# Splitting the last stage's weights during the mLSTM stage of a two-layer decoder trunk

## The chip, the core and the metric

The kernel runs on one core of a Trainium2 chip. The metric is the device time of one execution in microseconds (us). Three runs of the kernel before the change took 2989.78 to 2992.91 us, with a median of 2991.87.

A core has five engines that each work through a queue of their own: TensorE (PE in the profile; its weight loads are PEld), VectorE (DVE), ScalarE (ACT), GpSimd (POOL) and SyncE (SP), which here issues DMA transfers only. POOL issues DMA transfers too. An instruction that must wait holds up all that stands behind it on its engine.

## What is computed

One sequence of 2048 tokens with 1024 channels goes through two layers, `x = x + mixer(rmsnorm(x))`. The first mixer is an mLSTM (4 heads with a matrix memory), the second an RG-LRU (a gated linear recurrence of width 1536). The change concerns two weights of the second: the gates' block-diagonal matrices `w_a`, `w_x` (8 blocks of 192x192 each) and the output matrix `w_out`.

```python
def rglru_mixer(u, w_in, conv_w, conv_b, w_a, b_a, w_x, b_x, lam, w_out):
    xr, g = jnp.split(u @ w_in, [R_WIDTH], axis=-1)
    xc = causal_dwconv(xr, conv_w, conv_b)
    xb = xc.reshape(bsz, s, R_BLOCKS, R_BS)
    r = jax.nn.sigmoid(jnp.einsum('bsnc,ncd->bsnd', xb, w_a).reshape(bsz, s, R_WIDTH) + b_a)
    ig = jax.nn.sigmoid(jnp.einsum('bsnc,ncd->bsnd', xb, w_x).reshape(bsz, s, R_WIDTH) + b_x)
    log_a = -LRU_C * r.astype(jnp.float32) * jax.nn.softplus(-lam.astype(jnp.float32))
    bt = jnp.sqrt(-jnp.expm1(2.0 * log_a)) * (ig * xc).astype(jnp.float32)
    hs = linear_scan(jnp.exp(log_a), bt).astype(u.dtype)
    return (hs * jax.nn.silu(g)) @ w_out
```

## The kernel before

**Split operands.** Every large product is made of three passes on TensorE. An operand is split into a high part, a rounded copy, and a low part, the rest: `split_into` (lines 754 to 763) makes the high part by a cast on ScalarE (L759) and the low part by a subtract on VectorE (L762). The three passes are high by high (L359), low by high (L360) and high by low (L361).

**Stages.** The profile's span runs through four stages. Up to about 1000 us the mLSTM's input projections are made. From about 1000 to 1700 us `phase_a2` (line 773) computes the mLSTM: 4 heads after one another, each in 8 blocks of 256 tokens, some 21 us a block. From about 1670 to 2505 us `phase_b1` computes the output product of the first layer and the input product of the second. From 2505 us to the end `phase_b2` (line 1333) computes the RG-LRU's gates, its scan and its output product, in 4 blocks of 512 tokens.

**The mLSTM stage.** One pass of the main loop (lines 1036 to 1065) handles a block: the norm and finish of the block before it (`norm`, line 1012; `finish`, line 1018), the loads for the block after it, the recurrence over its own two chunks, and the projections to q, k and v of the block after it. The norm takes the factors `frs` from POOL (L1010), scales with them on ScalarE (`hh`, L1014), and TensorE transposes the result (`pt`, L1024). `head_weights` (lines 800 to 823) loads a head's weights for q, k and v as raw tiles (tag `wraw`, two slots, L807) and splits them. q's and k's for the next head are asked for at the end of blocks 3 and 5, v's with the next head's first block. Where a split stands in an engine's queue is decided by the scheduler, which merges these calls. In the order that comes out, the splits of q and k of the next head stand at the turn to it, where the splits of v stand too.

**The last stage.** A block has 8 gate steps of 18 matmuls (`gates`, line 1420) and, 5 steps behind, 24 output steps of 12 matmuls, 3 to each gate step (lines 1341 to 1346). Two gate steps serve a quarter of the block's 1536 channels. For a quarter ScalarE makes the sigmoids (L1435, L1438), the decay and its square (L1442, L1443) and, after the load of another function table, the root (L1463). VectorE makes the scan's input (L1466 to L1470), the scan (L1473) and the product with the branch `g` (L1476). Then the quarter of y is split (L759, L762) for the output steps. The x of a quarter is loaded by `load` (L1409) on SP and split in turn.

The weights come through `fetch` (lines 1353 to 1376). In the first block it loads raw tiles through POOL (L1363), splits them, and stores high and low part side by side to DRAM, `d_gw` for the gates and `d_ow` for the output (L1382, 32 stores). In the other three blocks it loads those stored parts through SP (L1360). Explicit orders put the split of the first gate weight ahead of the last work of the stage before, and the first x ahead of the first output weight. The gate pool has two slots for split tiles and two for raw ones, the output pool four and two.

Of the kernel before, what the change touches and what calls it, by code (L numbers as in the profile page):

```python
# [7 lines left out]
F32 = mybir.dt.float32  # L8
F32R = mybir.dt.float32r
# [5 lines left out]
P = 128  # L15
# [9 lines left out]
KV = DV // P  # L25
# [281 lines left out]
class Trunk:  # L307
# [462 lines left out]
                    self.tc.add_manual_dep(t.ins, f.ins.name, mybir.DependencyInfo(  # L770
                        mybir.DependencyClass.NoSync, mybir.DependencyReason.DATA), reason="order")

    def phase_a2(self, wq, wk, wv, D):
        tc, nc = self.tc, self.nc
        BL = 256
        NB = T // BL
        with ExitStack() as ctx:
            wp = ctx.enter_context(tc.tile_pool(name="w2", bufs=1, reuse_waits="tile"))
# [23 lines left out]
            def head_weights(h, names):  # L802
                w = W.setdefault(h, {})
                for nm in names:
                    src = {"q": wq[h], "k": wk[h], "v0": wv[h, :, :, 0:256], "v1": wv[h, :, :, 256:512]}[nm]
                    raw = wp.tile([P, KV, 256], F32, tag="wraw", name="wraw", bufs=2)
                    nc.sync.dma_start(raw, src)  # L807
                    if nm[0] == "v":
                        j = int(nm[1])
                        if j == 0:  # L810
                            w["v"] = (wp.tile([P, KV, 512], F32R, tag="vwh", name="vwh"),
                                      wp.tile([P, KV, 512], F32R, tag="vwl", name="vwl"))
                        hi, lo = (t[:, :, j * 256:(j + 1) * 256] for t in w["v"])
                    else:
                        pool = ob if h % 2 else wp
                        w[nm] = (pool.tile([P, KV, 256], F32R, tag=nm + "wh", name=nm + "wh"),
                                 pool.tile([P, KV, 256], F32R, tag=nm + "wl", name=nm + "wl"))
                        hi, lo = w[nm]
                    a = self.split_into(hi, lo, raw, "a", "v")
                    if h == 0 and nm[0] == "v":  # L820
                        self.order((self.kT,), a)
                    if h == 0 and nm in "qk":
                        self.order(a, self.tail[-4:])

            def project(h, b):

# [38 lines left out]
                def qk():  # L865
# [32 lines left out]
                    if b == 0:  # L898
                        head_weights(h, ("v0", "v1"))
# [112 lines left out]
            def norm(h, b, S):  # L1012
                rs = S["rs"]
                return [nc.scalar.activation(hn, hn, AF.Identity, bias=rs[:, 1, c:c + 1], scale=rs[:, 0, c:c + 1])  # L1014
                        for c, hn in enumerate(S["hh"])]

            def finish(h, b, S):
                y = lp.tile([P, KV, BL], F32, tag="y", name="y")
                for j in range(2):
                    pt = pr.tile([P, 2, 2, P], F32, tag="r", name="pt")  # L1020
                    for k in range(2):
                        for c in range(2):
                            ks = slice((j * 2 + k) * P, (j * 2 + k + 1) * P)
                            nc.tensor.transpose(pt[:, k, c], S["hh"][c][:, ks], self.ident)  # L1024
                    for k in range(2):
                        kk = j * 2 + k
                        a = nc.scalar.activation(y[:, kk], pt[:, k].rearrange("p c t -> p (c t)"), AF.Copy,
                                                 scale=self.v("nw", h * KV + kk))
                        if (h, b) == blocks[-1]:
                            self.tail.append(a)  # L1030
                nc.vector.tensor_tensor(y, y, S["skx"], op=ALU.add)
                end = (h, b) == blocks[-1]
                nc.vector.tensor_tensor(y, y, S["sz"], op=ALU.mult)
                (nc.sync if end else nc.gpsimd).dma_start(D["y"][h * KV:(h + 1) * KV, :, b * BL:(b + 1) * BL].rearrange("k p t -> p k t"), y)

            blocks = [(h, b) for h in range(H) for b in range(NB)]
            S, steps = project(*blocks[0])
            with tc.high_priority():
                steps[0]()
# [3 lines left out]
            for i, (h, b) in enumerate(blocks):  # L1043
                if i + 1 < len(blocks):
                    Sn, (loads, qk, score, v0, v1) = project(*blocks[i + 1])
                else:
                    Sn, loads = None, lambda: None
                    qk = score = v0 = v1 = loads
                if late:
                    norm(*late)  # L1050
                loads()
                recur(h, b, 0, S)
                if late:
                    finish(*late)
                qk()
                recur(h, b, 1, S)
                score()
                v0()
                v1()
                if b in (3, 5) and h < H - 1:  # L1060
                    head_weights(h + 1, "q" if b == 3 else "k")
                late = (h, b, S)
                S = Sn
            norm(*late)
# [20 lines left out]
                             start=True, stop=True)  # L1085
        return pb

    def phase_b(self, xT, wout, rwin, rgate, rwout, D, outT):
        self.phase_b1(xT, wout, rwin, D)
        self.phase_b2(rgate, rwout, D, outT)  # L1090

    def phase_b1(self, xT, wout, rwin, D):

# [236 lines left out]
                    S.group(W, U, out_of(i, s), {"t2": after_t2, "u21": after_u21})  # L1330
                    U, x1 = V, x3

    def phase_b2(self, rgate, rwout, D, outT):


        tc, nc = self.tc, self.nc
        NT = 12
        with ExitStack() as ctx:
            gp = ctx.enter_context(tc.tile_pool(name="g4", bufs=2, reuse_waits="tile"))
            tp = ctx.enter_context(tc.tile_pool(name="t4", bufs=2, reuse_waits="tile"))  # L1340
            wp = ctx.enter_context(tc.tile_pool(name="w4", bufs=4, reuse_waits="tile"))
            pm = ctx.enter_context(tc.tile_pool(name="psB", bufs=8, space=PSUM, reuse_waits="tile"))
# [10 lines left out]
            def fetch(kind, b, i):  # L1353

                m = 768 if kind == "g" else 512
                pool = gp if kind == "g" else wp
                keep = D["gw" if kind == "g" else "ow"][i]
                if b > 0:
                    both = pool.tile([P, 2 * m], F32R, tag="w" + kind, name="w" + kind)
                    nc.sync.dma_start(both.bitcast(F32), keep)  # L1360
                    return both[:, 0:m], both[:, m:2 * m]
                raw = pool.tile([P, m], F32, tag="wr" + kind, name="wr", bufs=2)
                nc.gpsimd.dma_start(raw, rgate[i // 2, :, i % 2 * 768:(i % 2 + 1) * 768] if kind == "g" else  # L1363
                                    rwout[i % NT, :, i // NT * 512:(i // NT + 1) * 512])
                kept(1)
                both = pool.tile([P, 2 * m], F32R, tag="w" + kind, name="w" + kind)
                a = self.split_into(both[:, 0:m], both[:, m:2 * m], raw, "a", "v")
                if kind == "g" and i == 0:
                    self.order(a, self.tail[-4:])
                if kind == "r" and i == 0:  # L1370
                    self.order(self.first, a)
                stores.append((keep, both))
                if i == (7 if kind == "g" else 23):
                    kept(0)
                return both[:, 0:m], both[:, m:2 * m]
            stores = []

            def kept(n):

                while len(stores) > n:  # L1380
                    keep, both = stores.pop(0)
                    nc.gpsimd.dma_start(keep, both.bitcast(F32))  # L1382

            def weights():

# [237 lines left out]
def trunk_kernel(tc, xT, woq, wxz, wq, wk, wv, wout, rwin, rgate, rwout, vecs, gbias, outT):  # L1623
    with ExitStack() as ctx:
        K = Trunk(ctx, tc, vecs, gbias)
        D = {}
        for n, shape in (("o", [NTC, P, MI]), ("xm", [16, P, T]), ("xc", [16, P, T]), ("sz", [16, P, T]),
                         ("y", [16, P, T]), ("x1", [KD, P, T]), ("xr", [12, P, T]), ("g", [12, P, T]), ("q", [64, P]), ("dec", [64, P]), ("wx", [16, 4, P, 1024]),
                         ("wq", [H, 4, 2, P, 1032]), ("wr", [12, 4, P, 1024]), ("ws", [4, 8, P, 1024]),
                         ("gw", [8, P, 1536]), ("ow", [24, P, 1024])):  # L1630
            D[n] = tc.dram_tile(shape, F32, name="d_" + n)
        K.phase_a1(xT, woq, wxz, wout, D)
        K.phase_a2(wq, wk, wv, D)
        K.phase_b(xT, wout, rwin, rgate, rwout, D, outT)


_INS = ["xT", "woq", "wxz", "wq", "wk", "wv", "wout", "rwin", "rgate", "rwout", "vecs", "gbias"]
# [22 lines left out]
```

## Time and profile before

| | us |
|---|---|
| median of three runs | 2991.87 |
| the profiled execution | 2996.22 |
| its span in the trace | 2994.5 |
| mLSTM stage, window shown below | 1020 to 1700 |
| first gate matmul of the last stage | 2509.48 |
| fourth cast of y in the last stage | 2617.98 |

The profile is of one execution, taken by the hardware's profiler. A grouped row gives the source line, the engine, the operation, the tiles out<-in with their shapes, the count, then the busy time, the mean duration in ns, and the idle time of the engine just before, with what ended it. A row of windows gives, for a stretch, the busy time of each engine with its number of instructions in brackets, the granted TensorE clock as a share of full speed, the share of the DMA engines' time in use, and GB/s. A busy time counts overlapping matmuls once. A row of waits gives who waited for whom, the time in all, how often, and the longest one. A row of transfers gives the tiles, the queue, the count, the KB of one and its median us from issue to landing.

### The profile page before, as it was taken

To read this page: it belongs to the slowest core of one execution; us is meant where nothing else is said; L and a number is where in the kernel's file an instruction comes from. 1 tells how busy PE (TensorE), PEld (TensorE's weight loads), DVE (VectorE), ACT (ScalarE), POOL (GpSimd) and SP (SyncE) were. 2 spreads that over 40 slices of the span, in tenths; PEclk is the share of its full clock that TensorE was granted. 3 is DMA by queue.
4 is the path that set the end of the run, shared out by engine and by line. 5 is a ranking of instruction groups with operands and counts; after the bars stand their busy time and mean duration, and the time that the engine had idled before them with its cause. 6 is when DMAs were issued, how large, how long until landed. Compare 5 with 4: busy or idle time off the path is not lost. (4 is left out here: it accounts for less than half of the span.)

```text
span 2994.5 us, 43193 instructions
## 1 busy us (share of the span) xinstructions
PE 2861.5 (96%) x15442; PEld 2448.8 (82%) x15442; DVE 2127.1 (71%) x3596; ACT 1517.2 (51%) x2557; POOL 455.6 (15%) x870
## 2 busy tenths in 40 slices
PE   7999999999999999999999899999999998699997
PEld 5799987899987798998999777887888886587885
DVE  7766788535568588888888666768888474766763
ACT  6344555324445566666666433435445234777761
POOL 1211122102123111111111101002221111210000
PEclk9999999999999999999999899999999998799998
DMA  6766677668889644445443767676766657778865
GB/s 226 265 225 240 233 252 251 209 200 299 287 299 312 210 144 156 144 136 164 132 148 124 255 218 267 217 238 221 246 228 213 217 178 252 261 278 299 299 205 170
DMA packets 289783, 667.70 MB, mean 223 GB/s; under 512 B 28576, under 2 KB 107168, under 8 KB 289568
## 3 DMA queue, kind: packets, MB, share of 16 engines
q1 hardware_dynamic: 219952, 422.03, 44.4%
q0 software_dynamic: 69040, 241.87, 21.3%
q8 instruction: 121, 1.98, 0.3%
q10 hardware_dynamic: 576, 1.05, 0.1%
q14 instruction: 94, 0.77, 0.1%
HBM read 427.66 MB, written 237.17 MB: 222 GB/s over the span
## 5 line engine op out<-in xcount | busy, mean ns | idle before, releaser
L759 ACT CAST s<-raw 128x512 fp32r<-128x512 f32 (+1 forms) x280 | 172.2, 620 | 262.1 <-PE pd L361 70.8
L762 DVE TENSOR_TENSOR s<-raw,s 128x512 fp32r<-128x512 f32 (+1 forms) x280 | 191.6, 689 | 64.3 <-ACT s L759 63.3
L359 PE MATMUL acc<-yh,wr 128*128 128x512 f32 x384 | 153.3, 406 | 22.2 <-DMA wr<-d_ow 8.1
L360 PE MATMUL acc<-yl,wr 128*128 128x512 f32 x384 | 154.8, 403 | 0.6 <-DVE yl L762 0.6
L361 PE MATMUL acc<-yh,wr 128*128 128x512 f32 x384 | 154.3, 402 | 0.0
L759 ACT CAST u<-t 128x512 fp32r<-128x512 f32 x112 | 68.8, 619 | 153.4 <-PE pc L361 50.6
L686 DVE SCALAR_TENSOR_TENSOR xc<-xm,vec,xc 128x512 f32<-128x512 f32 x192 | 139.2, 747 | 6.0 <-ACT xc L684 4.6
L762 DVE TENSOR_TENSOR u<-t,u 128x512 fp32r<-128x512 f32 x112 | 76.8, 690 | 84.5 <-ACT u L759 84.0
L759 ACT CAST s<-sum 128x512 fp32r<-128x512 f32 (+1 forms) x120 | 74.0, 618 | 116.8 <-PE pc L361 46.5
L359 PE MATMUL pa<-u,s 128*128 128x512 f32 x304 | 122.1, 401 | 4.7 <-ACT p L258 3.1
L361 PE MATMUL pa<-u,s 128*128 128x512 f32 x304 | 121.4, 400 | 0.1
L360 PE MATMUL pa<-u,s 128*128 128x512 f32 x304 | 121.5, 400 | 0.0
L759 ACT CAST Ch<-C 128x516 fp32r<-128x516 f32 x120 | 74.8, 623 | 85.2 <-DVE da L989 70.3
L971 DVE SCALAR_TENSOR_TENSOR C<-C,dl,kv 128x516 f32<-128x516 f32 x112 | 83.7, 747 | 47.3 <-PE kv L361 47.3
L686 DVE SCALAR_TENSOR_TENSOR xc<-xr,vec,xc 128x512 f32<-128x512 f32 x144 | 106.0, 748 | 9.2 <-ACT xc L684 8.4
L359 PEld LDWEIGHTS acc<-yh,wr 128*128 128x128 f32 x384 | 73.9, 194 | 42.7 <-ACT yh L759 8.8
L359 PE MATMUL pj<-vwh,xmh 128*128 128x512 f32 x256 | 102.6, 401 | 0.3 <-ACT vwh L759 0.3
L762 DVE TENSOR_TENSOR s<-sum,s 128x512 fp32r<-128x512 f32 (+1 forms) x120 | 82.6, 689 | 25.7 <-ACT s L759 24.7
L360 PE MATMUL pj<-vwl,xmh 128*128 128x512 f32 x256 | 99.8, 390 | 0.7 <-DVE vwl L762 0.7
L361 PE MATMUL pj<-vwh,xml 128*128 128x512 f32 x256 | 100.1, 391 | 0.0
L359 PE MATMUL gate<-xch,wg 128*128 128x512 f32 x192 | 78.3, 412 | 17.5 <-ACT xch L759 12.6
L360 PE MATMUL pd<-u,s 128*128 128x512 f32 x224 | 88.5, 395 | 2.0 <-DVE u L762 2.0
(483 smaller groups left out, 10061.9 us busy)
## 6 DMA issues: line engine op xcount, KB each, us to landing
wr<-d_ow SPq DMA_DIRECT2D x72, 512.0 KB, 4.3
d_wx<-s POOLq DMA_DIRECT2D x64, 512.0 KB, 4.4
s<-d_wx SPq DMA_DIRECT2D x64, 512.0 KB, 4.3
s<-d_ws SPq DMA_DIRECT2D x64, 512.0 KB, 6.1
raw<-in_wxz_dram SPq DMA_DIRECT2D x124, 256.0 KB, 4.8
d_wr<-s POOLq DMA_DIRECT2D x48, 512.0 KB, 3.6
s<-d_wr SPq DMA_DIRECT2D x48, 512.0 KB, 4.3
raw<-in_rwin_dram SPq DMA_DIRECT2D x94, 256.0 KB, 3.9
```

What stands on the lines that cost most here:

```text
L359: mm(out, sh, mh, start=first, stop=False, skip_group_check=resumed)
L360: mm(out, sh, ml, start=False, stop=False, skip_group_check=resumed)
L361: mm(out, sl, mh, start=False, stop=last, skip_group_check=resumed)
L686: nc.vector.scalar_tensor_tensor(out, x[:, j:j + TB], self.v(wn, m * 4 + j), out, op0=ALU.mult, op1=ALU.add)
L759: a = nc.scalar.copy(hi, src)
L762: b = (nc.gpsimd if lo_eng == "p" else nc.vector).tensor_tensor(lo, src, hi.bitcast(F32), op=ALU.subtract)
L971: nc.vector.scalar_tensor_tensor(C2, C2, self.dl[:, r:r + 1], p2, op0=ALU.mult, op1=ALU.add)
```

## The change

The last stage's weights are split during the mLSTM stage. A generator `later_weights` in `phase_a2` handles 20 parts: 8 half tiles of gate weights (128x768) and 12 tiles of output weights (128x1024, each of which fills two of the last stage's tiles). For a part it loads the raw weights through SP into one `wraw` slot, casts the high part into the other, subtracts in place, and stores both parts through POOL into `d_gw` or `d_ow`. The main loop takes one part at the end of blocks 1, 2, 4, 6 and 7 of each head. `fetch` in the last stage now loads stored parts through SP in all four blocks. The raw tiles, the splits and the stores of the first block are gone, with the two explicit orders. The gate pool has three slots, which take the room of its two and of its two raw ones.

```diff
-    def phase_a2(self, wq, wk, wv, D):
+    def phase_a2(self, wq, wk, wv, rgate, rwout, D):
...
+            def later_weights():
+
+                parts = [(rgate[i // 2, :, i % 2 * 768:(i % 2 + 1) * 768],
+                          [D["gw"][i, :, l * 768:(l + 1) * 768] for l in range(2)]) for i in range(8)]
+                parts += [(rwout[k], [D["ow"].rearrange("(h k) p (l n) -> k l p h n", h=2, l=2)[k, l] for l in range(2)])
+                          for k in range(12)]
+                for src, keep in parts:
+                    n = src.shape[-1]
+                    raw, hi = (wp.tile([P, KV * 256], F32, tag="wraw", name="wraw", bufs=2)[:, 0:n] for _ in range(2))
+                    nc.sync.dma_start(raw, src)
+                    self.split_into(hi.bitcast(F32R), raw.bitcast(F32R), raw, "a", "v")
+                    for t, k in zip((hi, raw), keep):
+                        nc.gpsimd.dma_start(k, t if n == 768 else t.rearrange("p (h n) -> p h n", h=2))
+                    yield
...
+            later = later_weights()
...
                 if b in (3, 5) and h < H - 1:
                     head_weights(h + 1, "q" if b == 3 else "k")
+                elif b in (1, 2, 4, 6, 7):
+                    next(later, None)
...
-            gp = ctx.enter_context(tc.tile_pool(name="g4", bufs=2, reuse_waits="tile"))
+            gp = ctx.enter_context(tc.tile_pool(name="g4", bufs=3, reuse_waits="tile"))
...
             def fetch(kind, b, i):
 
                 m = 768 if kind == "g" else 512
-                pool = gp if kind == "g" else wp
-                keep = D["gw" if kind == "g" else "ow"][i]
-                if b > 0:
-                    both = pool.tile([P, 2 * m], F32R, tag="w" + kind, name="w" + kind)
-                    nc.sync.dma_start(both.bitcast(F32), keep)
-                    return both[:, 0:m], both[:, m:2 * m]
-                raw = pool.tile([P, m], F32, tag="wr" + kind, name="wr", bufs=2)
-                nc.gpsimd.dma_start(raw, rgate[i // 2, :, i % 2 * 768:(i % 2 + 1) * 768] if kind == "g" else
-                                    rwout[i % NT, :, i // NT * 512:(i // NT + 1) * 512])
-                kept(1)
-                both = pool.tile([P, 2 * m], F32R, tag="w" + kind, name="w" + kind)
-                a = self.split_into(both[:, 0:m], both[:, m:2 * m], raw, "a", "v")
-                if kind == "g" and i == 0:
-                    self.order(a, self.tail[-4:])
-                if kind == "r" and i == 0:
-                    self.order(self.first, a)
-                stores.append((keep, both))
-                if i == (7 if kind == "g" else 23):
-                    kept(0)
+                both = (gp if kind == "g" else wp).tile([P, 2 * m], F32R, tag="w" + kind, name="w" + kind)
+                nc.sync.dma_start(both.bitcast(F32), D["gw" if kind == "g" else "ow"][i])
                 return both[:, 0:m], both[:, m:2 * m]
```

The scheduler puts the parts into the queues. At the turn from head 0 to head 1, ScalarE's queue before the change holds the casts of the next head's q and k weights (the number behind a name tells tiles of one name apart):

```order
L902 ACTIVATE skx_12202<-xc_12040,vec_58 128x256 x4
L759 CAST qwh_13376<-wraw_13374 128x1024
L896 COPY kT_12190<-pj_12165 128x512
L759 CAST xch_12306<-xc_12299 128x1024
L759 CAST qh_12161<-qd_12159 128x512
L759 CAST kwh_13928<-wraw_13926 128x1024
L925 ACTIVATE kh_12256<-kt_12251,wlT_75 128x256
L759 CAST sh_12247<-sm_12245 128x256
L871 ACTIVATE wgt_12651<-qb_12557,gT_74 128x128 x2
L939 CAST vh0_9950<-pj_12262 128x2x256
```

With the change the same place reads as follows, its own lines 15 further down (L759 is where it was):

```order
L917 ACTIVATE skx_12230<-xc_12068,vec_58 128x256 x4
L759 CAST wraw_12321<-wraw_12320 128x768
L911 COPY kT_12218<-pj_12193 128x512
L759 CAST xch_12341<-xc_12334 128x1024
L759 CAST qh_12189<-qd_12187 128x512
L940 ACTIVATE kh_12284<-kt_12279,wlT_75 128x256
L759 CAST sh_12275<-sm_12273 128x256
L886 ACTIVATE wgt_12686<-qb_12592,gT_74 128x128 x2
L759 CAST wraw_12864<-wraw_12863 128x768
L940 ACTIVATE kh_12284<-kt_12279,wlT_75 128x256
L954 CAST vh0_9950<-pj_12290 128x2x256
```

Two parts have taken the places of the casts of q and k, which now stand later in the head. The second one stands behind `wgt` and ahead of a cast of the keys and of the first cast of v, and it takes the slots of the first.

At the start of the last stage SP's queue holds, before the change, the last weights of `phase_b1` (`d_wr`), then x and g:

```order
L98 DMA s<-d_wr 128x1024 x12
L1409 DMA xc<-d_xr 128x3x512 x2
L1465 DMA g<-d_g 128x3x512
L1409 DMA xc<-d_xr 128x3x512
L1465 DMA g<-d_g 128x3x512
L1409 DMA xc<-d_xr 128x3x512
```

With the change it holds the stored weights as well:

```order
L98 DMA s<-d_wr 128x1024 x12
L1375 DMA wg<-d_gw 128x1536 x3
L1403 DMA xc<-d_xr 128x3x512 x2
L1459 DMA g<-d_g 128x3x512
L1375 DMA wr<-d_ow 128x1024
L1403 DMA xc<-d_xr 128x3x512
L1375 DMA wg<-d_gw 128x1536
L1375 DMA wr<-d_ow 128x1024
```

Three tiles of gate weights stand ahead of the first x on SP, where before the raw gate weights came through POOL.

More of the change, by code (lines that the diff above doesn't have):

```diff
@@ L1086, in stats_rows, with phase_b @@
         return pb
-    def phase_b(self, xT, wout, rwin, rgate, rwout, D, outT):
+    def phase_b(self, xT, wout, rwin, D, outT):
         self.phase_b1(xT, wout, rwin, D)
-        self.phase_b2(rgate, rwout, D, outT)
+        self.phase_b2(D, outT)
     def phase_b1(self, xT, wout, rwin, D):
@@ L1331, in phase_b1, with phase_b2 @@
                     U, x1 = V, x3
-    def phase_b2(self, rgate, rwout, D, outT):
+    def phase_b2(self, D, outT):
         tc, nc = self.tc, self.nc
@@ L1355, in fetch @@
                 m = 768 if kind == "g" else 512
-                pool = gp if kind == "g" else wp
-                keep = D["gw" if kind == "g" else "ow"][i]
-                if b > 0:
-                    both = pool.tile([P, 2 * m], F32R, tag="w" + kind, name="w" + kind)
-                    nc.sync.dma_start(both.bitcast(F32), keep)
-                    return both[:, 0:m], both[:, m:2 * m]
-                raw = pool.tile([P, m], F32, tag="wr" + kind, name="wr", bufs=2)
-                nc.gpsimd.dma_start(raw, rgate[i // 2, :, i % 2 * 768:(i % 2 + 1) * 768] if kind == "g" else
-                                    rwout[i % NT, :, i // NT * 512:(i // NT + 1) * 512])
-                kept(1)
-                both = pool.tile([P, 2 * m], F32R, tag="w" + kind, name="w" + kind)
-                a = self.split_into(both[:, 0:m], both[:, m:2 * m], raw, "a", "v")
-                if kind == "g" and i == 0:
-                    self.order(a, self.tail[-4:])
-                if kind == "r" and i == 0:
-                    self.order(self.first, a)
-                stores.append((keep, both))
-                if i == (7 if kind == "g" else 23):
-                    kept(0)
-                return both[:, 0:m], both[:, m:2 * m]
[L1376 to L1382, printed above, removed]
+                both = (gp if kind == "g" else wp).tile([P, 2 * m], F32R, tag="w" + kind, name="w" + kind)
+                nc.sync.dma_start(both.bitcast(F32), D["gw" if kind == "g" else "ow"][i])
+                return both[:, 0:m], both[:, m:2 * m]
             def weights():
@@ L1632, in trunk_kernel @@
         K.phase_a1(xT, woq, wxz, wout, D)
-        K.phase_a2(wq, wk, wv, D)
-        K.phase_b(xT, wout, rwin, rgate, rwout, D, outT)
+        K.phase_a2(wq, wk, wv, rgate, rwout, D)
+        K.phase_b(xT, wout, rwin, D, outT)
 _INS = ["xT", "woq", "wxz", "wq", "wk", "wv", "wout", "rwin", "rgate", "rwout", "vecs", "gbias"]
```

## The prediction

> **What bounds the kernel now.** I read the page first, then the stages by windows, then the waits and rows of two places: the first block of the last stage, which loses work, and the mLSTM stage, which takes it over.
>
> ```profile
> PE 2861.5 (96%) x15442; PEld 2448.8 (82%) x15442; DVE 2127.1 (71%) x3596; ACT 1517.2 (51%) x2557; POOL 455.6 (15%) x870
> ```
>
> TensorE is the bound on the average (the page, where the engines stand on five lines, is here read by its first row: 2861.5 us of the 2994.5 us span), so time can be won only where TensorE stands.
>
> ```profile
> core 0: us, PE busy (x) PEld busy (x) DVE busy (x) ACT busy (x) POOL busy (x), PEclk, DMA share, GB/s
> 2504.80:2620.00 115.20, 78.36 (x266) 57.56 (x266) 74.13 (x63) 85.47 (x110) 24.22 (x45) 0.79 0.80 287
> 2620.00:2720.00 100.00, 100.00 (x441) 81.46 (x440) 71.19 (x67) 75.77 (x98) 17.14 (x29) 1.00 0.79 276
> ```
>
> The last stage's first block stands out. The second row is the same stage running full: 441 matmuls in 100 us, 0.2268 us each. At that pace the 266 matmuls of the first row are 60.3 us of work, and they took 115.2: the first block **loses 54.9 us**, as idle time and as a clock of 0.79. What it waits for is ScalarE:
>
> ```profile
> L1435 ACT ACTIVATE R<-gate,lc 64x512 f32<-64x512 f32 (+1 forms) x19 | 12.8, 678 | 0.2
> L1438 ACT ACTIVATE ig<-gate,lc 64x512 f32<-64x512 f32 (+1 forms) x18 | 12.3, 681 | 0.3
> L1442 ACT ACTIVATE A<-R,lc 128x512 f32<-128x512 f32 x14 | 11.4, 811 | 0.1
> L1443 ACT ACTIVATE R<-R,lc 128x512 f32<-128x512 f32 x13 | 10.5, 810 | 0.0
> ...
> L759 ACT CAST wr<-wr 128x512 fp32r<-128x512 f32 x13 | 7.9, 615 | 8.2 <-PE gate L361 4.3 <-PE acc L361 2.6 <-DMA wr<-in_rwout_dram 1.2
> L759 ACT CAST wg<-wr 128x768 fp32r<-128x768 f32 x8 | 6.6, 826 | 19.5 <-DMA d_gw<-wg 11.2 <-DMA wr<-in_rgate_dram 7.8 <-PE gate L361 0.5
> L1463 ACT ACTIVATE R<-R 128x1536 f32<-128x1536 f32 x4 | 5.9, 1484 | 0.0
> L759 ACT CAST yh<-g 128x1536 fp32r<-128x1536 f32 x4 | 5.9, 1470 | 3.1 <-DVE g L1476 3.1
> L1463 ACT ACT_TABLE_LOAD x4 | 5.1, 1283 | 0.1
> ...
> L1475 ACT COPY hcarry<-xc 128x3 f32<-128x3 f32 x4 | 0.7, 185 | 4.3 <-DVE xc L1473 4.3
> ```
>
> This is ScalarE from 2500 to 2625, grouped by line (busy us, mean ns, idle before it and what ended it). Two of its groups are the splits of raw weights: 13 casts of output weights and 8 of gate weights, 14.5 us, with 27.7 us of idle in front of them (19.5 and 8.2). The gates' nonlinearities stand behind those casts in the same queue, and the fourth quarter of y, without which TensorE can't go on, comes late:
>
> ```profile
> 2512.75 0.69 ACT L1435 ACTIVATE R<-gate,lc 128x512 f32<-128x512 f32 x1
> ...
> 2617.98 1.48 ACT L759 CAST yh<-g 128x1536 fp32r<-128x1536 f32 x1 [3.12 <-DVE g L1476]
> ```
>
> From the first gate to the last cast of y of that block, 105 us pass.
>
> The mLSTM stage is another picture (windows, columns as above):
>
> ```profile
> 1020.00:1700.00 680.00, 654.72 (x4692) 614.84 (x4693) 555.78 (x1019) 429.75 (x823) 89.33 (x201) 0.98 0.46 149
> 1140.00:1160.00 20.00, 19.86 (x146) 18.68 (x145) 16.42 (x32) 12.79 (x26) 2.57 (x6) 1.00 0.42 127
> 1180.00:1200.00 20.00, 16.50 (x104) 15.14 (x103) 15.49 (x29) 12.04 (x23) 2.56 (x6) 0.91 0.64 213
> 1500.00:1520.00 20.00, 19.31 (x141) 18.17 (x142) 16.65 (x29) 14.74 (x28) 2.56 (x6) 1.00 0.40 138
> ```
>
> TensorE is 96% busy there, VectorE 82%, ScalarE 63%. A quiet block (second row) idles 0.14 us. The turn from head 0 to head 1 (third row), where the next head's q and k weights are split, is the exception.
>
> **The change in the last stage.** Its 32 splits go: 8 casts at 0.826 and 24 at 0.615 us on ScalarE, as many subtracts on VectorE, and 32 stores on GpSimd's queue. Most of this, and all of the waiting, is in the first block. What is late next is ScalarE's own gate chain. A quarter of a block is 8 activations of 0.68 (L1435, L1438), 6 of 0.81 (L1442, L1443), the root of 1.48, two table loads of 1.28, a cast of y of 1.47, one of the next x of about 1.47 (by the y row, as its shape is the same) and the carry of 0.19: 17.5 us. TensorE's share of a quarter is 36 matmuls, 8.2 us, so ScalarE sets the pace. Four quarters from 2512.75, the roots ending one chain behind their quarter, put the fourth root at about 2578, and from it the way to y lies on VectorE:
>
> ```profile
> L1473 DVE TENSOR_TENSOR_SCAN xc<-A,hcarry,R 128x512 f32<-128x512 f32 x12 | 14.6, 1268 | 0.0
> ...
> L762 DVE TENSOR_TENSOR wg<-wr,wg 128x768 fp32r<-128x768 f32 x8 | 7.6, 953 | 19.9 <-ACT wg L759 19.9
> ...
> L1466 DVE SCALAR_TENSOR_TENSOR R<-A,R 128x1536 f32<-128x1536 f32 x4 | 7.0, 1758 | 7.1 <-ACT R L1463 7.1
> ...
> L1476 DVE TENSOR_TENSOR g<-xc,g 128x1536 f32<-128x1536 f32 x4 | 7.0, 1753 | 0.0
> ...
> L1470 DVE TENSOR_TENSOR R<-R,xc 128x1536 f32<-128x1536 f32 x4 | 7.0, 1751 | 0.0
> ```
>
> That is 1.76 + 1.75 + 3 x 1.27 + 1.75 = 9.1 us, with some queueing 14: the fourth cast of y at about **2592 instead of 2618**, 26 us earlier. If TensorE uses the time to run one gate step (18 matmuls, 4.1 us) or more ahead, up to 33 us are won. I take **-30**. The ends: -15 if only the casts' own 14.5 us leave the queue and every wait finds another cause; -36 if the chain runs from 2512.75 without a gap (105 us less the 14.5 of casts and the 27.7 of idle is 63, but four quarters are 70, so 2582).
>
> What stays: the loads of the first x stand behind three kept gate tiles of 768 KB on SyncE's queue now, but those tiles wait only for products that end before x's own place is free, so they are issued earlier. I cost this at nothing; if x lands late by one landing of the rows below, it is 4 us.
>
> **The change in the mLSTM stage.** Twenty parts are added: 8 casts of 0.826 and 12 of 1.05 on ScalarE (19.2 us), 8 subtracts of 0.953 (the wg row above) and 12 of 1.218 on VectorE (22 us), 20 loads on SyncE and 40 stores on GpSimd.
>
> ```profile
> L759 ACT CAST kwh<-wraw x4: 1044/1046/1051, 994.1 to 1352.2; 128x1024 fp32r<-128x1024 f32 x4
> L762 DVE TENSOR_TENSOR kwl<-wraw,kwh x4: 1215/1218/1221, 999.3 to 1357.9; 128x1024 fp32r<-128x1024 f32 x4
> ```
>
> About 28 MB over 680 us are 42 GB/s on top of 149, below the 287 that the last stage moves: no term. In a quiet block ScalarE has 7 and VectorE 3.6 of 20 us free, so a split hides; I take **0.1 us** for each of 16 splits in such places (10 parts, and 6 splits of q and k that the new order moves out of the turns), by the 0.14 us of the quiet row: 1.6 us. What a split costs in a busy place, the turns show (TensorE's waits, 1160 to 1200, then 1500 to 1540):
>
> ```profile
> PE pt L1024 <- ACT hh L1014: 3.5, 2, 3.1
> PE n L359 <- DVE hh L994: 0.7, 1, 0.7
> ```
> ```profile
> PE n L359 <- DVE hh L994: 1.1, 2, 0.7
> ```
>
> The first turn has v's splits and those of q and k, the second v's alone: 4.2 against 1.1, so two more splits cost 3.1 us there. In the new order two parts stand at each turn. At the first two turns they take the places of q and k; at the third they are new: **+3.1**.
>
> Then there is a new wait. Raw and high tile of a part take the two slots that the heads' own weights use. The next part's load waits until the high tile's store has landed, its cast for that load and for the low tile's store.
>
> ```profile
> d_y<-y POOLq DMA_DIRECT2D x31, 512.0 KB, 6.8
> ...
> wraw<-in_wq_dram SPq DMA_DIRECT2D x4, 512.0 KB, 4.1
> ```
>
> From one cast to the next that is 0.83 + 6.8 + 4.1 = 11.7 us. ScalarE comes to the next cast earlier at five places. The first and the last of the five are, by the rows beside which the casts are put (behind skx, behind wgt):
>
> ```profile
> 1176.88 1.71 ACT L902 ACTIVATE skx<-xc,vec 128x256 f32<-128x256 f32 x4 [0.94 <-DVE y L1031]
> ...
> 1183.58 0.69 ACT L871 ACTIVATE wgt<-qb,gT 128x128 f32<-128x128 f32 x2
> ...
> 1536.07 1.30 ACT L902 ACTIVATE skx<-xc,vec 128x256 f32<-128x256 f32 x3
> ...
> 1544.02 0.68 ACT L871 ACTIVATE wgt<-qb,gT 128x128 f32<-128x128 f32 x2
> ```
>
> The distances, end to end, are 5.7 and 7.3 us; the other three are 8.0, 7.8 and 5.8. ScalarE would stand 6.0, 4.4, 3.7, 3.9 and 5.9, together 24 us, with the key and value casts that TensorE needs queued behind it; on GpSimd the stores wait for the same splits, and the next norm's frs stands behind them. The row of the third turn leaves ScalarE 5.3 us of 20 free, so I take half of the standing: **+12**. The ends: nothing, if that slack covers it, and 24 whole plus 1.55 us (half of 3.1) for each of the ten other parts, 40 in all. For the sum: 12 + 3.1 + 1.6 = **+17**, from 0 to 40.
>
> By the Trainium skill, "DMA: Bandwidth & Descriptors", section "Anatomy of one DMA — SWDGE (gpsimd) path", a store from GpSimd takes about 2.0 us and its bytes over 436 KB per us. For 384 KB that would be an estimated 2.9 us and a chain of 7.8 us, so that only the two closest pairs would stand about 2 us each. The d_y row of this very stage says 6.8 us for 512 KB, over twice the 3.2 of that rule, and so speaks against it here.
>
> **The sum.** The profiled execution took 2996.22 us, 1.7 around its span of 2994.5. 2996.2 - 30 + 17 = 2983, and since the median of the three runs is 4.35 below it, **2979**.
>
> **The rivals.**
>
> *Slower: the two slots hold up every pair.* If the standing reaches TensorE whole and a split costs 1.55 us everywhere, the mLSTM stage grows by 40. The row 1180:1200 shows what follows a wait of 3 us: the granted clock falls to 0.91, 1.8 us of 20, and three more such places make 45. With -30 that is **3007**. It decides as soon as the stage grows by over 36, 1.8 us a part. For it: VectorE at 82% and the 4.2 us of the first turn. Against it: the quiet rows.
> By the Trainium skill, "TensorE: Matmul & The Clock Gate", section "Part 1: The HAM clock gate (the "warmup" mystery)", an idle window of about 3.4 us halves the clock. The trace agrees in part: 0.91 where one wait was 3.1 us, 1.00 where the waits were under 1.
>
> *The first block stays late.* With the casts gone, the gates could wait for x, for the 9.1 us of VectorE or for the g loads instead: -15, with +17 in the other stage **2994**, no change. For it: 0.80 of the transfer time is taken in that block. Against it: half of that traffic, the raw loads and stores, goes.
>
> *The stores land sooner.* Another stage's stores of the same size from the same queue do:
>
> ```profile
> d_wr<-s POOLq DMA_DIRECT2D x48, 512.0 KB, 3.6
> ```
>
> The chain is then 8.5 us, the standing 2.8, 1.2, 0.5, 0.7 and 2.7, 8 us, half of it 4; with 3.1 and 1.6 the stage grows by 9: **2971**. The rule on stores cited above would give about the same, an estimated 2969.
>
> **How the numbers follow.** Forecast 0.50, sooner landing 0.18, first block late 0.17, slower 0.15. A measurement of this kernel tells about 0.2%, 6 us, from no change. The first two lie outside on the fast side: faster 0.68; the third gives same 0.17; the last slower 0.15. The range runs from 2960 (-36 and +4) to 3000, short of the slower case's own value, as the steps between 2979 and 3007 hold most of its chance.
>
> **What would show it.** In the changed profile: the matmuls of the last stage's first 115 us (266 before; near 400 by a gain of 30, under 332 by one below 15); the time from first gate to fourth cast of y (80 us, not 105); no cast of wg or wr there; ScalarE's waits on d_gw and d_ow stores or on raw loads at the five places (10 to 24 us right, none the sooner landing); TensorE's waits and clock at the turns; and the length of the mLSTM stage, +17. I am wrong if that stage grows by over 36 or not at all, or if the first block gains under 15.

## The result, and the profile after

The changed kernel takes 3014.86 us (median of 4 runs, 3012.82 to 3017.94) against 2991.57 us before (2989.78 to 2992.91, 4 runs): a ratio of 1.0079, with a 95% interval from 1.0062 to 1.0097. It is slower by 23 us where 2979 us and a gain were forecast. Its profiled execution took 3013.40 us, with a span of 3011.5.

```profile
PE 2868.1 (95%) x15442; PEld 2455.6 (82%) x15442; DVE 2126.0 (71%) x3584; ACT 1515.3 (50%) x2545; POOL 456.2 (15%) x846
```

TensorE, the first item of the page's first row, does the same 15442 matmuls in a span that is 17 us longer. The span splits at three events: the mLSTM stage from its first block's last product on VectorE to that of its last block (`y<-y,sz`), the stretch from there to the first gate matmul, and the last stage from that matmul to the end. First the rows of before, by tile (count, shortest, median and longest ns, first and last start):

```profile
L1033 DVE TENSOR_TENSOR y<-y,sz x32: 1205/1216/1225, 1051.8 to 1696.8; 128x1024 f32<-128x1024 f32 x32
...
L359 PE MATMUL gate<-xch,wg x192: 388/392/795, 2509.5 to 2917.1; 128*128 128x512 f32 x192
```

and the same of after:

```profile
L1048 DVE TENSOR_TENSOR y<-y,sz x32: 1190/1214/1225, 1047.3 to 1748.4; 128x1024 f32<-128x1024 f32 x32
...
L359 PE MATMUL gate<-xch,wg x192: 388/392/796, 2561.3 to 2934.3; 128*128 128x512 f32 x192
```

| | before, us | after, us | difference | forecast |
|---|---|---|---|---|
| up to the first block's product | 1051.8 | 1047.3 | -4.5 | 0 |
| mLSTM stage | 645.0 | 701.1 | **+56.1** | +17 |
| to the first gate matmul | 812.7 | 812.9 | +0.2 | 0 |
| last stage | 485.0 | 450.2 | **-34.8** | -30 |
| span | 2994.5 | 3011.5 | +17.0 | -13 |

The first row is what one execution differs from another: over all profiles below, that event lies between 1044.7 and 1053.0. The spans differ by 17 us and the medians by 23, because the profiled execution before was 4.6 us slower than its median and the one after 1.5 us faster than its own.

The last stage did what it was meant to. Its first 115 us and the 100 us behind them, by windows with the columns of before:

```profile
2556.60:2671.80 115.20, 102.14 (x412) 79.12 (x411) 78.39 (x58) 96.00 (x119) 0.54 (x1) 0.96 0.83 289
2671.80:2771.80 100.00, 99.10 (x437) 80.36 (x436) 70.53 (x60) 69.83 (x87) 6.31 (x9) 1.00 0.79 281
```

412 matmuls instead of 266, at a clock of 0.96 instead of 0.79. The first activation of the gates and the four casts of y on ScalarE, in order of time:

```profile
2564.92 0.68 ACT L1429 ACTIVATE R<-gate,lc 128x512 f32<-128x512 f32 x1
...
2589.24 1.48 ACT L759 CAST yh<-g 128x1536 fp32r<-128x1536 f32 x1 [0.30 <-DVE g L1470]
...
2606.71 1.48 ACT L759 CAST yh<-g 128x1536 fp32r<-128x1536 f32 x1 [0.30 <-DVE g L1470]
...
2622.65 1.47 ACT L759 CAST yh<-g 128x1536 fp32r<-128x1536 f32 x1 [0.30 <-DVE g L1470]
...
2642.22 1.47 ACT L759 CAST yh<-g 128x1536 fp32r<-128x1536 f32 x1
```

The casts stand 16 to 20 us apart, by the 17.5 us that a quarter costs ScalarE; the fourth ends 79 us after the first gate, where 81 were forecast and 107 were seen before.

So the loss is in the mLSTM stage. The times from one block's product to the next show where (each is the distance between two starts of `y<-y,sz`):

| head, block | 0,1 | 0,2 to 0,6 | 0,7 | 1,0 | 1,1 | 1,2 to 1,6 | 1,7 | 2,0 | 2,1 | 2,2 to 2,6 | 2,7 | 3,0 | 3,1 | 3,2 to 3,7 |
|---|---|---|---|---|---|---|---|---|---|---|---|---|---|---|
| before | 21.0 | 105.8 | 20.4 | 23.2 | 21.0 | 105.7 | 19.9 | 23.3 | 21.0 | 105.7 | 16.8 | 22.4 | 21.0 | 117.6 |
| after | 27.5 | 106.1 | 25.2 | 26.4 | 28.1 | 106.0 | 23.7 | 29.0 | 23.8 | 107.3 | 23.6 | 28.5 | 27.5 | 118.3 |

Most blocks lose nothing at all. Those at and behind a turn lose 3 to 7 us each (the product of a head's last block is made in the first pass of the next head). The parts are asked for all along a head, but the scheduler puts them early, so that four to six of them, with the splits of q and k for the next head, stand in the two to four passes at a head's start. They wait there. ScalarE's waits of that stage, and then the only one of over 0.3 us that a cast of q or k had before the change:

```profile
ACT wraw L759 <- DMA wraw<-in_rwout_dram: 15.9, 6, 5.1
...
ACT wraw L759 <- DMA wraw<-in_rgate_dram: 10.4, 4, 6.5
...
ACT qwh L759 <- DMA wraw<-in_wq_dram: 10.0, 3, 5.6
...
ACT wraw L759 <- DMA d_ow<-wraw: 7.4, 2, 6.1
...
ACT kwh L759 <- DMA wraw<-in_wk_dram: 5.5, 2, 2.8
```
```profile
ACT kwh L759 <- DMA wraw<-in_wk_dram: 1.5, 1, 1.5
```

ScalarE stands 49.2 us in 17 casts that wait for a slot's load or store; before, the casts of q and k waited under 2 us in all. One such wait, at the turn to head 1, on ScalarE and on SyncE's queue:

```profile
1180.86 0.82 ACT L759 CAST wraw<-wraw 128x768 fp32r<-128x768 f32 x1
...
1192.90 0.83 ACT L759 CAST wraw<-wraw 128x768 fp32r<-128x768 f32 x1 [6.54 <-DMA wraw<-in_rgate_dram]
1193.63 0.47 ACT L940 ACTIVATE kh<-kt,wlT 128x256 fp32r<-128x256 f32 x1
1194.00 0.58 ACT L954 CAST vh<-pj 128x512 fp32r<-128x512 f32 x1
```
```profile
1183.42 0.33 SPq L853 DMA_DIRECT2D db<-d_dec  x1
1188.37 0.34 SPq L834 DMA_DIRECT2D wraw<-in_rgate_dram  x1
1188.82 0.50 SPq L851 DMA_DIRECT2D qb<-d_q  x1
```

The second part's load is issued at 1188.37, once its slot is free, with the q rows behind it. That slot held the first part's high tile, whose store, issued at 1181.97, took 6.3 us to land, up to 1188.3:

```profile
L837 POOL DMA_DIRECT2D d_gw<-wraw x1: 637/637/637, 1182.0 to 1182.0; - x1
...
DMA to landing us min/median/max: 6.3/6.3/6.3
```

The second part's cast begins 12.0 us after the first part's, and `kh` and `vh`, which TensorE needs, come behind that. TensorE's longest waits in the stage, the same three before the change, then its wait and its window at this place:

```profile
PE pt L1039 <- ACT hh L1029: 20.3, 10, 6.4
PE kv L359 <- ACT vh L954: 15.3, 6, 4.5
PE kv L359 <- DVE C L986: 10.3, 11, 2.9
```
```profile
PE pt L1024 <- ACT hh L1014: 11.3, 5, 4.8
...
PE kv L359 <- DVE C L971: 3.5, 15, 0.6
...
PE kv L359 <- ACT vh L939: 0.8, 1, 0.8
```
```profile
PE kv L359 <- ACT vh L954: 4.2, 1, 4.2
```
```profile
1180.00:1200.00 20.00, 14.10 (x76) 12.00 (x75) 14.27 (x28) 9.76 (x18) 5.55 (x10) 0.86 0.76 244
```

In those 20 us TensorE does 76 matmuls, at a mean clock of 0.86; the same window, at nearly the same place in the work, had 104 before. What the waits cost beside their length shows in the whole stage, between the two products, before and after:

```profile
1051.80:1696.80 645.00, 621.88 (x4467) 584.75 (x4466) 526.74 (x969) 410.54 (x789) 85.47 (x192) 0.98 0.46 148
```
```profile
1047.30:1748.40 701.10, 642.59 (x4486) 601.17 (x4486) 548.59 (x990) 426.72 (x808) 118.16 (x226) 0.96 0.53 174
```

TensorE idles 58.5 us where it idled 23.1, which is 35 of the 56 us. The other 21 are busy time: nearly the same matmuls take longer, at a mean clock of 0.96 instead of 0.98.

### The profile page after: what moved, and what is told of

It reads as the page before. It is cut to its first block, busy times and chain, and to the rows that moved or that the text cites. A ratio compares the mean times of both kernels' runs of the same rounds, so it can differ in the third digit from the quotient of the medians.

```text
span 3011.5 us, 43205 instructions
## 1 busy us (share of the span) xinstructions
PE 2868.1 (95%) x15442; PEld 2455.6 (82%) x15442; DVE 2126.0 (71%) x3584; ACT 1515.3 (50%) x2545; POOL 456.2 (15%) x846
## 5 line engine op out<-in xcount | busy, mean ns | idle before, releaser
L759 ACT CAST s<-raw 128x512 fp32r<-128x512 f32 (+1 forms) x280 | 172.1, 620 | 259.9 <-PE pd L361 69.3
L759 ACT CAST u<-t 128x512 fp32r<-128x512 f32 x112 | 68.8, 619 | 154.1 <-PE pc L361 51.0
L759 ACT CAST s<-sum 128x512 fp32r<-128x512 f32 (+1 forms) x120 | 74.1, 618 | 115.8 <-PE pc L361 44.3
L686 DVE SCALAR_TENSOR_TENSOR xc<-xr,vec,xc 128x512 f32<-128x512 f32 x144 | 106.0, 748 | 9.2 <-ACT xc L684 7.9
L759 ACT CAST Ch<-C 128x516 fp32r<-128x516 f32 x120 | 74.7, 623 | 65.9 <-DVE da L1004 52.5
L359 PE MATMUL kv<-vh,kh 128*128 128x258 f32 x240 | 73.8, 307 | 26.4 <-ACT vh L954 15.3
```

The source lines that it names most:

```text
L359: mm(out, sh, mh, start=first, stop=False, skip_group_check=resumed)
L686: nc.vector.scalar_tensor_tensor(out, x[:, j:j + TB], self.v(wn, m * 4 + j), out, op0=ALU.mult, op1=ALU.add)
L759: a = nc.scalar.copy(hi, src)
```

## The experiments

Each row is one kernel, with the median of 4 to 11 executions (of 2 for no_store, no_split and pin_loads). The last two columns are stage lengths of one profiled execution each, in us, by the events of the first table; the ratio is against the kernel before on the same chip.

| run | median, us | ratio to before (95%) | mLSTM stage against before | last stage |
|---|---|---|---|---|
| parts_only | 3050.28 | 1.0195 (1.0178 to 1.0212) | +51.4 | 484.5 |
| pinned | 3024.64 | 1.0110 (1.0095 to 1.0125) | +66.5 | 449.9 |
| no_store | 3014.25 | 1.0076 (1.0056 to 1.0096) | +23.1 | 486.2 |
| no_split | 3023.50 | 1.0107 (1.0086 to 1.0127) | +21.7 | 484.0 |
| pin_all | 2994.16 | 1.0007 (0.9997 to 1.0016) | +34.9 | 450.2 |
| pin_casts | 2999.58 | 1.0026 (1.0016 to 1.0037) | +44.7 | 450.1 |
| pin_loads | 2972.75 | 0.9938 (0.9918 to 0.9958) | +17.3 | 449.5 |
| no_split_pin | 2986.23 | 0.9981 (0.9971 to 0.9992) | -5.7 | 484.2 |
| spread | 2969.31 | 0.9923 (0.9909 to 0.9936) | +11.3 | 450.1 |
| spread_b | 2963.16 | **0.9904** (0.9889 to 0.9919) | +4.9 | 449.9 |
| before_pin | 2986.57 | 0.9976 (0.9967 to 0.9985) | -4.8 | 485.1 |

The last column takes two values only: about 485 where the last stage splits raw weights, 450 where it reads stored parts. Everything else in this table happens in the mLSTM stage.

**parts_only.** The parts are made as in the changed kernel, by the same generator, and `phase_b2` is that of before.

```diff
             blocks = [(h, b) for h in range(H) for b in range(NB)]
+            later = later_weights()
...
+                elif b in (1, 2, 4, 6, 7):
+                    next(later, None)
```

> The 20 parts are split and stored in the mLSTM stage as in the changed kernel, and the last stage is that of before (it splits raw weights itself and stores them again). All theories: the mLSTM stage grows by what the changed profile shows, 55 us, and the last stage stays at that of before, so 2991.6 + 55 = 3047 us. If the time is under 3030, part of the 55 us belongs to the changed last stage.

It took 3050.28 us, 59 us more than before, 3 more than expected; the mLSTM stage grew by 51 us in the profiled execution, the stretch behind it by 5. The loss comes with the parts, and the two halves of the change don't act on each other.

**pinned.**

```diff
-                    self.split_into(hi.bitcast(F32R), raw.bitcast(F32R), raw, "a", "v")
+                    a = self.split_into(hi.bitcast(F32R), raw.bitcast(F32R), raw, "a", "v")
+                    self.order((self.kT,), a)
```

> The changed kernel, with each part's cast ordered behind the kT copy of the block that is being projected when the part is asked for, so that the parts stand a block or more apart instead of bunched behind the turns. Theory A (bunched parts wait for each other's stores and loads on the two slots, ScalarE stands and TensorE with it): the chain of 12 us fits between them, the mLSTM stage grows by 10 us or less, 2958 to 2968 us. Theory B (the work of a split costs TensorE some 2.8 us wherever it stands, 55 us for 20): the place doesn't matter, about 3015 us.

It took 3024.64 us, worse than the changed kernel: neither theory. The casts of the parts, now half a block or more apart, don't wait. But the casts of q and k use the same slots, and the scheduler has them taken some 7 us behind a part, where they wait:

```profile
1083.17 1.04 ACT L759 CAST qwh<-wraw 128x1024 fp32r<-128x1024 f32 x1 [6.11 <-DMA wraw<-in_wq_dram]
...
1129.05 1.05 ACT L759 CAST kwh<-wraw 128x1024 fp32r<-128x1024 f32 x1 [3.73 <-DMA wraw<-in_wk_dram]
```

And one block of the last head took 27 us though no cast waited in it. There the wait is on SyncE's queue. SyncE, GpSimd and ScalarE in that block:

```profile
1629.39 0.98 SPq L854 DMA_DIRECT2D db<-d_dec  x1
1637.43 0.34 SPq L834 DMA_DIRECT2D wraw<-in_rwout_dram  x1
1637.88 0.43 SPq L852 DMA_DIRECT2D qb<-d_q  x1
```
```profile
1642.32 0.41 POOL L883 TENSOR_SCALAR_AFFINE_SELECT qb<-qb 128x256 f32<-128x256 f32 x1 [8.29 <-DMA qb<-d_q]
1642.83 0.19 POOL L1023 TENSOR_SCALAR frs<-mv 128x2 f32<-128x2 f32 x1
```
```profile
1644.32 0.81 ACT L1030 ACTIVATE hh<-hh,frs 128x512 f32<-128x512 f32 x1 [5.83 <-POOL frs L1026]
```

The next part's load waits on SyncE until its slot is free, the small load of the q rows waits behind it, GpSimd waits for those rows with the norm's factors `frs` behind them, and `hh` on ScalarE waits for the factors. So theory A was right in what waits and wrong in where: every queue that touches a slot holds up what stands behind.

**no_store and no_split.** Both are parts_only with one side of a part left out: the first has no stores, so the parts are thrown away; in the second nothing is split, and each raw tile is stored twice.

```diff
-                    for t, k in zip((hi, raw), keep):
-                        nc.gpsimd.dma_start(k, t if n == 768 else t.rearrange("p (h n) -> p h n", h=2))
```
```diff
-                    self.split_into(hi.bitcast(F32R), raw.bitcast(F32R), raw, "a", "v")
-                    for t, k in zip((hi, raw), keep):
+                    for t, k in zip((raw, raw), keep):
```

> As parts_only, but the 40 stores of the parts are left out: the parts are loaded and split, and thrown away. Theory A: a slot comes free after the subtract, the chain is cast and load, 5 us instead of 12, and ScalarE stands a third as long: the stage grows by 5 to 20 us, 2997 to 3012 us. Theory B (the split's work): 3040 us or more. Theory C (the stores on GpSimd's queue hold up the norm's factors, or their traffic the loads): 2992 to 2997, as nothing of it is left.

> As parts_only, but the 20 casts and 20 subtracts of the parts are left out: each raw tile is loaded and stored twice, as it is. Theory A: no cast waits on the chain but those of q, k and v, so the stage grows by 15 us at most, up to 3007 us. Theory B: no growth, 2992 us. Theory C: most of the 55 us stay, 3025 us or more.

Without stores the stage grows by 23 us, without splits by 22. The first, at 3014 us, is just above theory A's range (to 3012); the second, at 3023.5, is far above A's (to 3007) and just short of theory C's 3025. Its growth points to a queue and not to the traffic, as it lies in the blocks at the turns to heads 1, 2 and 3 alone, one of them 30.8 us long. GpSimd and ScalarE there:

```profile
1563.20 1.43 POOL L836 DMA_DIRECT2D d_ow<-wraw  x2 [7.45 <-DMA wraw<-in_rwout_dram]
1568.56 1.45 POOL L836 DMA_DIRECT2D d_ow<-wraw  x2 [3.92 <-DMA wraw<-in_rwout_dram]
1570.09 0.18 POOL L1021 TENSOR_SCALAR frs<-mv 128x2 f32<-128x2 f32 x1
```
```profile
1571.94 1.52 ACT L1028 ACTIVATE hh<-hh,frs 128x512 f32<-128x512 f32 x2 [9.82 <-POOL frs L1024]
```

Here the third queue is the victim: GpSimd's stores wait for their loads with the norm's factors behind them. The two halves add up to 45 of parts_only's 51 us. How the 56 us of the changed kernel divide among the three queues can't be read from these two runs more closely than that.

**pin_all, pin_casts, pin_loads.** Theory D says that the root is one, the two slots, and that the queues are its victims. The loads and casts of the parts and of the later heads' q and k are pinned behind fixed instructions of the block being projected; pin_all has both pins, the others one each.

```diff
-                    nc.sync.dma_start(o, D["o"][b * 2:b * 2 + 2, :, h * DV:(h + 1) * DV].rearrange("c p n -> p c n"))
+                    self.ld = nc.sync.dma_start(o, D["o"][b * 2:b * 2 + 2, :, h * DV:(h + 1) * DV].rearrange("c p n -> p c n"))
...
-                    nc.sync.dma_start(raw, src)
+                    d = nc.sync.dma_start(raw, src)
+                    self.order((self.ld,), (d,))
...
+                    self.order((self.kT,), a)
```

> As pinned, and now the raw loads too: each part's load, and those of q and k of the next heads, stand on SyncE's queue behind the o load of the block being projected, and the casts of q and k behind its kT copy like those of the parts. Theory D (one root, two queues: whatever waits for one of the two slots holds up what stands behind it, casts on ScalarE and loads on SyncE, where the q rows, GpSimd's norm factors and then ScalarE's hh wait in turn): only v's loads at the turns still stand behind a part's stores, the mLSTM stage grows by 15 us at most, 2958 to 2973 us. Theory A (only casts on ScalarE matter): as pin_casts. Theory B (the work itself): 3015 us or more.

> As pin_all, but with the casts pinned alone; the loads stand where the scheduler puts them, early. Theory A: as pin_all, within 5 us, as no cast comes before its slot is free. Theory D: loads that wait for slots still hold up SyncE's queue, so 10 to 35 us above pin_all.

> As pin_all, but with the loads pinned alone; a cast can't be taken before its load, so casts are spread as well, though a cast may stand close behind its load. Theory D: 0 to 20 us above pin_all, by ScalarE's waits for loads just issued. Theory A: about as pinned, 3020 us, as casts still wait.

With the loads pinned alone the kernel is faster than before for the first time: 2972.75 us, with 17 us of growth in the stage. With both pins it is 2994.16, and with casts alone 2999.58. So theory A fell, as a pin of the loads does what a pin of the casts doesn't, and theory B with it, as the same 20 splits cost far less here. But D's three numbers missed too: pin_all was to take 2973 us at most, pin_casts 10 to 35 us more than pin_all (it takes 5 more) and pin_loads 0 to 20 more (it takes 21 less). A pin on the casts, added to that on the loads, makes things worse where I thought that it would help. GpSimd's waits for the q rows in this stage, of the kernel before, of pin_all and of pin_loads, point to a reason (us in all, times, longest):

```profile
POOL qb L867 <- DMA qb<-d_q: 52.1, 26, 8.5
```
```profile
POOL qb L888 <- DMA qb<-d_q: 100.0, 24, 9.7
```
```profile
POOL qb L885 <- DMA qb<-d_q: 45.8, 28, 6.9
```

A cast pinned behind `kT` comes some 10 us later than it could (the first part's at 1048.5 instead of 1038.6), so its slots come free later, and the next load holds SyncE's queue, and the q rows in it, for longer. No run tried this by itself.

**no_split_pin.** As no_split, with the loads pinned.

> As no_split (raw tiles loaded and stored twice, no cast, no subtract, last stage as before), with the loads of parts, q and k pinned as in pin_all. Theory D: the 22 us that the mLSTM stage of no_split grew were SyncE's queue behind loads that wait for slots, so at most 8 us are left of them: 2992 to 3010 us. Theory C (traffic, or the stores on GpSimd's queue): as no_split, 3020 us or more.

2986.23 us. All of the 22 us are gone, with the same loads, the same stores and the same bytes, so neither the traffic nor the time to issue stores was the cause. The stage is even 6 us shorter than before the change, about what the pin of q and k gains alone (before_pin, next).

**before_pin.** The kernel before, with nothing but the pin of q's and k's loads.

```diff
+                    if h > 0 and nm in "qk":
+                        self.order((self.ld,), (d,))
```

> The kernel before, with nothing changed but that the loads of q and k of the next heads are pinned as in pin_loads, which moves their splits out of the turns. By no_split_pin, whose mLSTM stage was 5 us shorter than that of before, 2985 to 2989 us. If so, the 20 parts of pin_loads cost 17 + 5 = 22 us, 1.1 us each, without waits for slots; if it stays at 2992, they cost 17, 0.9 us each.

2986.57 us: the stage is 4.8 us shorter, and q's and k's splits no longer stand at the turns beside v's. If that gain is in pin_loads too, its 20 parts cost 17.3 + 4.8 = 22 us.

**spread and spread_b.** pin_loads, with the parts asked for elsewhere.

```diff
-                elif b in (1, 2, 4, 6, 7):
+                elif b in (0, 1, 2, 4) or h == H - 1:
```
```diff
-                elif b in (1, 2, 4, 6, 7):
+                elif b in (0, 1, 2, 4, 6):
```

> As pin_loads, but the parts are asked for at blocks 0, 1, 2 and 4 of the first three heads and at all eight blocks of the last, so that no part stands close ahead of the loads of v at a turn and never two in a block. Theory D: the 1.4 to 4 us that pin_loads still loses at each turn and in the last two blocks go, the mLSTM stage grows by 8 to 14 us over before, 2964 to 2970 us. If each split costs about 1 us of TensorE wherever it stands, and the waits are gone already in pin_loads, it stays at 2971 to 2975 us.

> As spread, but with the parts at blocks 0, 1, 2, 4 and 6 of each head: a part at block 6 stands close ahead of v's loads. Theory D: 3 to 6 us more than spread; the split's own cost: the same as spread.

In the stage both beat pin_loads; in time spread isn't clear of it, as the intervals overlap. spread_b is the fastest kernel of this study: 2963.16 us, 0.96% faster than before. Its parts cost 4.9 + 4.8 = 9.7 us by the stages of single executions, 0.5 each; by the ratios (0.9904, 0.9976 for before_pin, and 35 us gained in the last stage) it is about 13 us, 0.7 each. The expectation that a part at block 6 costs 3 to 6 us was wrong, as spread_b takes 6 us less than spread: that block takes 23.0 us instead of 21.6, the next is as short as without it. What spread loses instead is at the end of the stage, where the last two parts have no block between them:

```profile
1657.12 1.05 ACT L759 CAST wraw<-wraw 128x1024 fp32r<-128x1024 f32 x1
...
1667.96 1.04 ACT L759 CAST wraw<-wraw 128x1024 fp32r<-128x1024 f32 x1 [2.81 <-DMA d_ow<-wraw]
```

This is the disputed wait by itself: two casts 10.8 us apart, a stand of 2.81 us on ScalarE, and a block of 27.1 us, which takes 22.9 in spread_b, with one part less there.

All these runs move loads and casts. None gave the parts slots of their own, so that the shared slots are the root is read from the waits and not shown by a run.

## Why the prediction was wrong

**What bounds the kernel, and the last stage: right.** -34.8 us were measured for -30, inside the range of -15 to -36 and a little over the 33 us that it gave as the most by this chain. Of the 54.9 us that the first block lost, 33 came back with the splits gone: at 0.2268 us each, the 412 matmuls are 93.4 of the 115.2 us. The load of x behind three gate tiles cost nothing that shows: TensorE waits for `xch` once, 4.4 us, where it waited twice and 12.6 us before.

**The chain on the two slots: right, with its size at four of five places.** 11.7 us from cast to cast were forecast; at the five close pairs the measured distances are 8.3, 12.0, 12.7, 12.6 and 11.9 us, and ScalarE stood 2.2, 6.5, 5.2, 5.0 and 4.3 us, together 23 where 24 were forecast. The medians of the stores look as if the third rival had been right and they landed sooner than the row that I took them from:

```profile
d_y<-y POOLq DMA_DIRECT2D x31, 512.0 KB, 6.9
...
d_ow<-wraw POOLq DMA_DIRECT2D x24, 512.0 KB, 4.2
...
d_gw<-wraw POOLq DMA_DIRECT2D x16, 384.0 KB, 3.3
```

But the chain doesn't run on the median. In all five pairs the next load is issued within 0.2 us of the landing of the high tile's store, and these five stores took 3.9, 6.3, 5.9, 6.3 and 6.6 us: the 6.8 that I took was about right at four of the five, and the third rival fell there. At those four a store of `d_y` was under way in the same queue, at the first there was none; that this is why they took longer wasn't tried. By the Trainium skill, "DMA: Bandwidth & Descriptors", section "Anatomy of one DMA — SWDGE (gpsimd) path", an estimated 2.9 and 3.2 us were to be expected for 384 and 512 KB; the medians of 3.3 and 4.2 come near that, the stores of the four pairs and the d_y row don't.

**The term of +17 for the mLSTM stage: wrong, and here the forecast failed.** It measured +56, through three steps.

- "I take 0.1 us for each of 16 splits in such places", 1.6 us in all. Those 16, the ten other parts and the six splits of q and k, are no quiet splits: they use the same two slots, and the scheduler bunches most of them behind the turns. Their casts stood 24 of the 49 us, 15.5 of them in q and k alone (10.0 and 5.5 in the rows above). The prediction followed the slots at five places of the old trace and took the rest as free, though every wait moves what comes behind it.
- "so I take half of the standing": with 24 us of standing that was +12, and nothing for the clock. Beside 49 us of standing on ScalarE, TensorE idled 35 us more than before and was busy 21 us longer at a lower clock. The slack of a block didn't absorb waits that fell ahead of `vh` or `kh`. How much of the 35 came by ScalarE and how much by the other two queues, the runs don't part.
- The waits on GpSimd's queue were named ("on GpSimd the stores wait for the same splits, and the next norm's frs stands behind them") but had no price, and the q rows behind a waiting load on SyncE's queue weren't named. no_split, which has no cast of a part, measures 22 us for them, and 0 or less once the loads are pinned.

The upper end of that term, 40, rested on the first step as well, so the range to 3000 was too narrow. The slower rival (the slots hold up every pair, and the clock falls behind the waits) had the right mechanism and, at 3007, came nearest; its condition, a growth by over 36 us, held. Its 1.55 us for a split wherever it stands did not, as the next paragraph shows. Its chance of 0.15 was too low: following the slots through all 26 casts in the new order would have shown more than five that wait.

**What the split itself costs** is small, as forecast, though not as small: 0.5 to 0.7 us for a part in spread_b, 10 to 13 us for all 20, against 2 us by the price of 0.1.

## What to carry to other kernels

Work moved into the slack of a busy stage needs room of its own or distance, of which only distance was tried here: where it shares rotating buffers with work that is on the path, each stand for a buffer holds up whatever is behind it in every queue that touches the buffer, loads and stores included. A scheduler that takes work as early as it can will put all of it in one place, so give each piece a place by its load, and leave a block between two pieces. Before costing such a move, follow the buffers through every piece in the new order, the old users of the buffers too, and let each wait shift the rest.

## What the runs showed of the hardware that was not expected

Two stores of 512 KB from GpSimd's queue in the same stage differ by much, in the median 6.9 us for `d_y`, whose runs in memory are 1 KB, and 4.2 for `d_ow`, whose runs are 2 KB. Where no other store of that queue was under way, it is 6.9 (`d_y` issued at 1098.03) against 3.2 (`d_ow` issued at 1590.13); beside a `d_y` store, a `d_ow` store took 5.9 to 6.6 at the three pairs above. Neither cause was tried by itself.

And TensorE's waits cost more than their length: in the mLSTM stage it idled 35 us more than before and needed 21 us more for nearly the same matmuls, at a mean granted clock of 0.96 instead of 0.98.
